# An expert stage's overflow branch, its scratch, four extra TensorE products and a table load change places in a two-layer MoE trunk

## The chip, the cores and the metric

The kernel runs on one core of a Trainium2 chip. The metric is the device time of one execution in microseconds; a profile of one execution shows each engine's instructions: TensorE (PE, with its weight loads as PEld), VectorE (DVE), ScalarE (ACT), GpSimd (POOL) and SyncE (SP), which here issues the weight transfers.

## The reference

256 tokens of 1024 numbers pass two layers. A layer is a token mixer (a gated depthwise convolution in the first, a chunked retention in the second), a norm, a mixture of 32 experts and another norm. All is float32. The part that the change touches is the mixture:

```python
grp_prob = softmax(xt @ w_grp + b_grp); p_g, g_idx = top_k(grp_prob, 1)      # 4 groups
exp_logits = (xt @ w_route + b_route).reshape(T, 4, 8)
sel = exp_logits of the chosen group; top_val, top_idx = top_k(sel, 2)
gates = softmax(top_val) * p_g
combine = sum(one_hot(g_idx * 8 + top_idx) * gates)                          # T x 32
for e in range(32):
    h = silu(xt @ w_gate[e]) * (xt @ w_up[e])                                # 1024 -> 512
    y = y + combine[:, e:e + 1] * (h @ w_down[e])                            # 512 -> 1024
x = layer_norm(alpha * x + y)
```

## The kernel before

Weights stream from memory in pieces of 1 MB (128 x 2048 float32), each into a slot of a ring of 12 or of a few other homes. The class that keeps them issues a load on SP as soon as a home is free: `take()` hands the next piece to the products, `used(n)` gives the homes of the n oldest pieces back and calls `load()` (L127 issues a whole piece, L112 one in halves). The engines' orders are those in which the code is written; nothing is moved by a scheduler.

An expert stage goes as follows. The routing (up to L1003) finds for each token its two experts. Three products, `pos` (L999 to L1001), give each token's place in its expert's list, with room for 64 tokens per expert. `one_hots` (L1043) makes from it, for four experts at a time, a selecting matrix on DVE. `gather` (L1057) multiplies it with the tokens, which are held as two parts `x1h` and `x1l`; four gathers make up the tokens of four experts, copied by ACT to `xghi` (gathers 0, 1) and `xglo` (gathers 2, 3). For each expert e `gate_up(e, i)`, i = 0 to 3, called product (e, i) here, does a quarter of both products (L1071, eight passes of 512 columns) into one accumulator `gu`; (e, 0) and (e, 1) read one pair of pieces, (e, 2) and (e, 3) the next. `hidden(e)` makes silu on ACT (L1080) and the product on DVE (L1082), `turn(e)` transposes the result on PE (L1091) and ACT copies it (L1104), `down` (L1126) multiplies with the third matrix, `parts` scales by the gates (ACT L1146, DVE L1147), and `scatter` (L1158) adds to the output rows. These steps of earlier experts are run between the products of later ones.

The list of an expert has 64 places. If one had more tokens, a second pass would be needed: `overflow`. `rest()`, called behind gathers 0 and 1, finishes the gates on DVE and returns `turned()`, called behind gathers 2 and 3: it transposes the places (`posT`, L1026) and, with a product (L1028), a sum and a cast on DVE (L1031, L1032), writes the number of tokens without a place to `flag`. `extra()`, called behind (0, 3), loads this number into a register of every engine (L1203) and opens `tc.If(rv > 0)` (L1208) around `overflow`. With the inputs of this kernel no list overflows, so the branch is never taken into the block. Its scratch are two ring slots (`spare`), and for their sake (0, 3) gives its two homes back only behind the branch. ACT then scales `cur`, the residual (L1228).

`warm(n, after)` (L302, L304) issues n bf16 products of 128 x 512 into a spare accumulator that nobody reads; `WARM` lists the n for eight places, and the sixth (`WARM[5]`, ahead of the gather) is 0. `preload(f)` (L361) calls a function of ACT on one column, so that ACT's function table is loaded ahead of its use; for the root it stands ahead of the norm that ends the stage.

Of the kernel before, what the change touches and what calls it, by code (L numbers as in the profile page):

```python
# [18 lines left out]
P = 128  # L19
# [14 lines left out]
T4 = 9  # L34
SPLIT = 4
ROWS_AT = [(27, 0), (27, 2), (28, 0), (28, 2)]
WARM = [11, 8, 8, 0, 2, 0, 1, 2]
YB = 2
TAPS_PE = [2, 2, 2, 2, 2, 2, 2, 14]
TAPS_POOL = [11, 12, 11, 8, 12, 11, 12, 7]  # L40
# [9 lines left out]
class Weights:  # L50
# [4 lines left out]
    def __init__(self, nc, ringp, splitp, handp, pieces, layers):  # L55
        self.nc, self.ringp, self.splitp, self.handp = nc, ringp, splitp, handp
        self.pieces, self.layers = pieces, layers
        self.next = 0
        self.tiles, self.parts = {}, {}
        self.order = [2 * i + j for i, (_, sp) in enumerate(pieces) if sp for j in range(2)]  # L60
        self.nsplit = 0
        self.nused = 0
        self.at = 0
        self.between = []
        self.stop = len(pieces)
        self.room = {"ring": RING, "own": 0, "split": 0, "once": 0}
        self.taken = []
        self.own = None

    def home(self, i):  # L70
        for a, b in self.layers:
# [19 lines left out]
    def load(self, n=99):  # L91

        for _ in range(n):
            while self.next in self.tiles:
                self.next += 1
            for i in range(self.next, len(self.pieces)):
                home, kind = self.home(i)
                if i not in self.tiles and (self.room[home] or home != "once"):
                    break
            else:  # L100
                return
            if not self.room[home]:
                return
            self.room[home] -= 1
            src = self.pieces[i][0]
            dma = self.nc.sync.dma_start
            if home == "split" or kind:
                m = src.shape[1] // 2
                v = []
                for h, tag in enumerate(("hd", "hd") if kind == "hand" else ("hi", "lo")):  # L110
                    t = (self.handp if kind == "hand" else self.splitp).tile([P, m, 1024 // m], F32, tag=tag, name=f"w{i}{h}")
                    dma(t, src[:, h * m:(h + 1) * m])  # L112
                    v += [t[:, k] for k in range(m)]
                self.tiles[i] = v
                continue
            t = (self.own if home == "own" else self.ringp).tile([P, 2048], F32, tag=home, name=f"w{i}",
                                                                 bufs=2 if home == "own" else RING)
            if isinstance(src, list):
                v = t.rearrange("p (g a b) -> p g a b", g=2, b=P)
                for g in range(2):  # L120
                    dma(v[:, g], src[g])
                    if self.between:
                        self.between.pop(0)()
                v = [v[:, g] for g in range(2)]
            else:
                v = t.rearrange("p (a b) -> p a b", a=src.shape[1])
                dma(v, src)  # L127
                if not self.pieces[i][1]:
                    v = [v[:, k] for k in range(src.shape[1])]
            self.tiles[i] = v  # L130
# [32 lines left out]
        t, self.tiles[i] = self.tiles[i], None  # L163
        return t

    def spare(self, name):

        t = self.ringp.tile([P, 2048], F32, tag="ring", name=name, bufs=RING)
        return t[:, 0:1024], t[:, 1024:2048]

    def used(self, n=1):

# [14 lines left out]
def trunk(ctx, tc, a, out):  # L187
# [18 lines left out]
    def sm1(name, dt=F32):  # L206
        return psum.tile([P, 512], dt, tag="sm", name=name, bufs=4)
# [740 lines left out]
    def route(L, ep, lg, comb, posm, posT, flag):  # L948
# [3 lines left out]
        def words(n):  # L952
            used[0] += n
            return space[:, used[0] - n:used[0]]

        def t2(n):
            t = words(2 * n)
            return t.rearrange("p (a b) -> p a b", a=2) if n > 1 else t

        def t2b():  # L960

            return words(NE).bitcast(BF).rearrange("p (a b) -> p a b", a=2)
# [43 lines left out]

        def rest():

            pg = t2(1)
            V.tensor_reduce(pg, gs, op=OP.add, axis=AX.X)  # L1010
            g1 = t2(1)
            V.scalar_tensor_tensor(g1, ex, 1.0, pg, op0=OP.add, op1=OP.mult)
            V.reciprocal(g1, g1)
            V.tensor_tensor(ex, ex, g1, op=OP.mult)
            V.tensor_tensor(oh1, oh1, bc(g1, 32), op=OP.mult)
            V.tensor_tensor(oh2, oh2, bc(ex, 32), op=OP.mult)
            V.tensor_tensor(comb, oh1, oh2, op=OP.add)
            posb = t2b()
            V.tensor_copy(posb, posm)
            over = t2b()  # L1020
            V.tensor_scalar(over, posm, CAP + 1.0, None, op0=OP.is_ge)

            def turned():
                pt = sm1("posT", BF)
                for tt in range(2):
                    PE.transpose(pt[:NE, tt * P:(tt + 1) * P], posb[:, tt], identb)  # L1026
                fp = sm1("flag")
                PE.matmul(fp[:1, 0:64], onesb[:, 0:1], over.rearrange("p a b -> p (a b)"), start=True, stop=True)  # L1028
                V.tensor_copy(posT, pt[:NE, :T])
                ff = words(1)[:1]  # L1030
                V.tensor_reduce(ff, fp[:1, 0:64], op=OP.add, axis=AX.X)  # L1031
                V.tensor_copy(flag, ff)  # L1032

            return turned

        mark["rest"] = rest

    def experts(L, mp, ep, x1h, x1l, comb, posm, posT, flag):
# [22 lines left out]
        def gate_up(e, i):  # L1061

            if i == 0:
                gus[e] = acc1(f"gu{e}")
            if i % 2 == 0:
                gws[e] = W.take(), W.take()
            for k in range(2):
                kt = i * 2 + k
                l = xg[e // 4][kt // 4][:, kt % 4, e % 4 * CAP:(e % 4 + 1) * CAP]
                for m, w in enumerate(gws[e]):  # L1070
                    PE.matmul(gus[e][m * CAP:(m + 1) * CAP], l, w[i % 2 * 2 + k], start=kt == 0, stop=kt == KT - 1)  # L1071
            if i % 2:
                gws.pop(e)
                if (e, i) != (0, 3):
                    W.used(2)

        def hidden(e):
            gu = gus.pop(e)
            gl = ep.tile([P, 512], F32, tag="gl", name=f"gl{e}")[CAP:]
            S.activation(gl, gu[:CAP], AF.Silu)  # L1080
            hs[e] = ep.tile([P, 4, P], F32, tag="h", name=f"h{e}")[CAP:]
            V.tensor_tensor(hs[e].rearrange("s k p -> s p k"), gl.rearrange("s (p k) -> s p k", k=4),  # L1082
                            gu[CAP:].rearrange("s (p k) -> s p k", k=4), op=OP.mult)
# [117 lines left out]
        def extra():  # L1201

            rv = nc.values_load(flag[0:1, 0:1], min_val=0, max_val=T * NE)  # L1203
            (wts, big), mid = [W.spare(f"ov{n}{L}") for n in range(2)]
            mid = [ep.tile([P, 512], F32, tag="gl", name="ovgl")[:CAP], *[m[:CAP] for m in mid]]
            row = ep.tile([P, T], F32, tag="s0", name="ovs", bufs=2)
            pair = [acc1(f"ov{n}") for n in range(2)]
            with tc.If(rv > 0):  # L1208
                overflow(L, x1h, x1l, comb, posm, wts, big, mid, row, pair)
        fin, seeds = {}, {}  # L1210
        identr = ep.tile([P, P], F32R, name="identr")
        G.tensor_copy(identr, ident)
        W.stop = layers[L][1]
        one_hots(0)
        warm(WARM[5])
        gather(0, range(2))
        turned = mark["rest"]()
        for e in range(NE):
            for i in range(4):
                gate_up(e, i)  # L1220
                if e == 0 and i == 0:
                    gather(0, range(2, 4))
                    turned()
                if e == 0 and i == 3:
                    extra()
                    W.used(2)
                    for tt in range(2):
                        S.activation(cur[:, tt], cur[:, tt], AF.Copy, scale=ALPHA)  # L1228
                if i == 3:
                    hidden(e)  # L1230
                run(e, i)
                if e + 4 < NE and e % 4 == 1 and i == 0:
                    one_hots(e // 4 + 1)
                if e + 2 < NE and e % 4 == 2:
                    gather(e // 4 + 1, [i])
                if (e, i) in ROWS_AT:
                    n = ROWS_AT.index((e, i))
                    if n == 0:
                        rows = mp.tile([P, 2048], F32, tag="x1h", name=f"rows{L}")
                    spread_rows(L, rows, n)  # L1240
            if L == 0 and e == 3:
                mark["rot"] = rotary_tables()
            if L == 0 and e == 10:
                mark["rot"]()
# [139 lines left out]
```

## Time and profile before

| | us |
|---|---|
| three runs | 1291.44, 1292.09, 1296.46 |
| median | 1292.09 |
| profiled execution | 1292.11 |
| its span | 1290.4 |
| PE busy | 1246.8 (97%) |
| DVE busy | 490.5 (38%) |
| ACT busy | 338.7 (26%) |

The profiled execution is the one whose rows are used; 1.7 us of its time lie outside the span. The mean granted TensorE clock was 0.98 of full speed. The two expert stages run from about 138 to 600 us and from about 821 to 1284 us. A table of stretches gives for each the engines' busy time, the granted clock and the share of the DMA engines; a timeline gives an engine's instructions with the idle time before each and what ended it.

### The profile page before, as it was taken

To read this page: it belongs to the slowest core of one execution; us is meant where nothing else is said; L and a number is where in the kernel's file an instruction comes from. 1 tells how busy PE (TensorE), PEld (TensorE's weight loads), DVE (VectorE), ACT (ScalarE), POOL (GpSimd) and SP (SyncE) were. 2 spreads that over 40 slices of the span, in tenths; PEclk is the share of its full clock that TensorE was granted. 3 is DMA by queue.
4 is the path that set the end of the run, shared out by engine and by line. 5 is a ranking of instruction groups with operands and counts; after the bars stand their busy time and mean duration, and the time that the engine had idled before them with its cause. 6 is when DMAs were issued, how large, how long until landed. Compare 5 with 4: busy or idle time off the path is not lost.

```text
span 1290.4 us, 15546 instructions
## 1 busy us (share of the span) xinstructions
PE 1246.8 (97%) x6163; PEld 659.6 (51%) x6163; DVE 490.5 (38%) x863; ACT 338.7 (26%) x561; POOL 139.9 (11%) x167
## 2 busy tenths in 40 slices
PE   9989899999999999998999999899999999999996
PEld 7867444343443334434997788544443444444432
DVE  5986313222232222235566755413222232222224
ACT  4655311121111111123434543411111211111111
POOL 4882008100000000002130000000000000000000
PEclk9999799999999999998999999899999999999998
DMA  9935699999999999999865556699999999999993
GB/s 321 398 116 175 224 391 426 425 425 425 424 427 425 425 425 425 426 427 409 290 197 180 179 196 197 261 382 405 422 425 426 425 427 425 425 426 424 427 426 137
DMA packets 102390, 459.45 MB, mean 356 GB/s; under 512 B 8258, under 2 KB 25442, under 8 KB 59554
## 3 DMA queue, kind: packets, MB, share of 16 engines
q1 hardware_dynamic: 102082, 457.92, 88.2%
q8 instruction: 53, 0.87, 0.3%
q0 software_dynamic: 80, 0.26, 0.1%
q10 hardware_dynamic: 144, 0.15, 0.1%
q14 instruction: 31, 0.25, 0.0%
HBM read 457.25 MB, written 1.05 MB: 355 GB/s over the span
## 4 chain that ended last, share of the span: by engine, by line
PE 60%; DMA 25%; DVE 2%; ACT 1%; issue 0%; DVEq 0%; SPq 0%; ACTq 0%
PE gu L1071 22%; DMA w<-in_moe_w_up_dram 11%; DMA w<-in_moe_w_down_dram 11%; PE y L1126 10%; PE gp L1057 4%; PE sc L1158 3%; DMA w<-in_moe_w_gate_dram 2%; PE vg L788 2%; PE vg L790 2%; PE vg L789 2%; PE hT L1091 1%; PE qk L771 1%; PE qk L770 1%; PE qk L768 1%; PE wo L656 1%; PE wo L657 1%
## 5 line engine op out<-in xcount | busy, mean ns | idle before, releaser
L1071 PE MATMUL gu<-w,xghi 128*64 128x512 f32 x1024 | 250.5, 606 | 1.9 <-DMA w<-in_moe_w_up_dram 1.0
L1126 PE MATMUL y<-w,h 128*64 128x512 f32 x960 | 240.9, 596 | 7.5 <-DMA w<-in_moe_w_down_dram 7.4
L1071 PE MATMUL gu<-w,xglo 128*64 128x512 f32 x1024 | 242.6, 600 | 0.0
L1082 DVE TENSOR_TENSOR h<-gl,gu 64x512 f32<-64x512 f32 x64 | 67.7, 1058 | 368.4 <-ACT gl L1080 368.4
L1126 PEld LDWEIGHTS y<-w,h 128*64 128x64 f32 x960 | 73.4, 137 | 151.8 <-issue 134.2
L1071 PEld LDWEIGHTS gu<-w,xglo 128*64 128x64 f32 x1024 | 69.7, 137 | 117.5 <-issue 107.9
L1071 PEld LDWEIGHTS gu<-w,xghi 128*64 128x64 f32 x1024 | 67.8, 137 | 110.4 <-issue 101.2
L143 DVE TENSOR_TENSOR l<-w,h 128x1024 fp32r<-128x1024 f32 x66 | 83.6, 1269 | 68.7 <-ACT h L142 67.1
L142 ACT ACTIVATE h<-w 128x1024 fp32r<-128x1024 f32 x72 | 75.7, 1058 | 88.0 <-PE vg L790 31.7
L1080 ACT ACTIVATE gl<-gu 64x512 f32<-64x512 f32 x64 | 37.7, 589 | 229.0 <-PE gu L1071 229.0
L1104 ACT ACTIVATE h<-hT 128x256 f32<-128x256 f32 x64 | 24.7, 385 | 261.3 <-PE hT L1101 148.9
L1162 DVE TENSOR_TENSOR cur<-sc,cur 128x512 f32<-128x512 f32 x112 | 69.5, 683 | 19.0 <-PE sc L1158 19.0
L1113 DVE COPY gsl<-hT 64x1 f32<-64x1 f32 x60 | 9.4, 156 | 169.8 <-ACT h L1104 169.4
L1057 PE MATMUL gp<-oh,x1h 128*128 128x256 f32 x256 | 59.0, 313 | 3.7 <-DVE route L1010 3.7
L1057 PEld LDWEIGHTS gp<-oh,x1h 128*128 128x128 f32 x256 | 40.5, 196 | 40.5 <-issue 39.6
L1146 ACT ACTIVATE yh<-y,gsl 128x512 fp32r<-128x512 f32 x60 | 41.2, 687 | 75.8 <-PE y L1126 75.6
L466 PE MATMUL pw<-xT,w 128*128 128x256 f32 x256 | 57.8, 381 | 1.6 <-DMA w<-in_conv_w_pw_dram 1.6
L499 POOL TENSOR_TENSOR gp<-gp,gt 128x256 f32<-128x256 f32 x76 | 56.3, 742 | 22.0 <-ACT gt L498 16.6
L143 POOL TENSOR_TENSOR l<-w,h 128x1024 fp32r<-128x1024 f32 x6 | 14.9, 2516 | 364.1 <-ACT h L142 364.1
L466 PEld LDWEIGHTS pw<-xT,w 128*128 128x128 f32 x256 | 48.2, 190 | 8.9 <-issue 2.5
L1057 PE MATMUL gp<-oh,x1l 128*128 128x256 f32 x256 | 52.6, 288 | 0.0
L1139 DVE TENSOR_SCALAR s<-sp,cc 128x256 fp32r<-128x256 f32 x30 | 14.5, 484 | 86.0 <-PE sp L1136 86.0
(322 smaller groups left out, 1585.1 us busy)
## 6 DMA issues: line engine op xcount, KB each, us to landing
w<-in_moe_w_up_dram SPq DMA_DIRECT2D x116, 1024.0 KB, 15.8
w<-in_moe_w_down_dram SPq DMA_DIRECT2D x112, 1024.0 KB, 17.1
w<-in_moe_w_gate_dram SPq DMA_DIRECT2D x106, 1024.0 KB, 14.7
w<-in_ret_w_qkvg_dram SPq DMA_DIRECT2D x24, 1024.0 KB, 13.2
w<-in_moe_w_gate_dram SPq DMA_DIRECT2D x44, 512.0 KB, 14.7
w<-in_moe_w_down_dram SPq DMA_DIRECT2D x32, 512.0 KB, 17.2
w<-in_moe_w_up_dram SPq DMA_DIRECT2D x24, 512.0 KB, 17.2
w<-in_conv_w_pw_dram SPq DMA_DIRECT2D x16, 512.0 KB, 6.3
```

What stands on the lines that cost most here:

```text
L142: self.nc.scalar.activation(hi, w, AF.Copy)
L143: (self.nc.gpsimd if pool else self.nc.vector).tensor_tensor(lo, w, hi.bitcast(F32), op=OP.subtract)
L466: PE.matmul(ps[:, 1 - g], w[g][:, kt], xT[:, kt], start=kt == 0, stop=kt == KT - 1)
L499: G.tensor_tensor(gps[c], gps[c], t, op=OP.add)
L1057: PE.matmul(ps[:, k], src[:, tt, q * 2 + k], o[:, tt].rearrange("p e c -> p (e c)"), start=i == 0, stop=i == 3)
L1071: PE.matmul(gus[e][m * CAP:(m + 1) * CAP], l, w[i % 2 * 2 + k], start=kt == 0, stop=kt == KT - 1)
L1080: S.activation(gl, gu[:CAP], AF.Silu)
L1082: V.tensor_tensor(hs[e].rearrange("s k p -> s p k"), gl.rearrange("s (p k) -> s p k", k=4), gu[CAP:].rearrange("s (p k) -> s p k", k=4), o ...
L1126: PE.matmul(ys[pr][b][j * CAP:(j + 1) * CAP], hs[e][:, kt], wds[e][kt % 2][:, n * 512:(n + 1) * 512], start=kt == 0, stop=kt == 3)
L1146: S.activation(yh[:, n], ys[pr][n], AF.Copy, scale=g)
L1158: PE.matmul(ps, s0[pr][ks, tt * P:(tt + 1) * P], ys[pr][i][ks, n if pr >= 0 else 0], start=not held and i == 0, stop=i == 1 and (pr == -1 ...
L1162: V.tensor_tensor(o, ps, o, op=OP.add)
```

## The change

`WARM[5]` goes from 0 to 4. The sum for the flag, `over`, is made first in `rest()`, the flag's product is a function of its own (`flagged`), called right behind gather 0, and `extra()` with the branch stands behind gathers 1 and 2, ahead of product (0, 0). Gather 3 and the transposes of the places follow (0, 1). The scratch is no longer two fresh slots but three homes whose pieces are already loaded (`lend`); inside the branch, after `overflow`, these pieces are read again. (0, 3) gives its homes back at once. A `preload(AF.Sqrt)` is added behind the last `hidden`.

```diff
-WARM = [11, 8, 8, 0, 2, 0, 1, 2]
+WARM = [11, 8, 8, 0, 2, 4, 1, 2]
...
-    def spare(self, name):
-
-        t = self.ringp.tile([P, 2048], F32, tag="ring", name=name, bufs=RING)
-        return t[:, 0:1024], t[:, 1024:2048]
+    def lend(self, n):
+
+        held = sorted(i for i, v in self.tiles.items() if v is not None and i in self.raw)[-n:]
+        return [self.raw[i] for i in held]
...
+            over = t2b()
+            V.tensor_scalar(over, posm, CAP + 1.0, None, op0=OP.is_ge)
             pg = t2(1)
...
-            over = t2b()
-            V.tensor_scalar(over, posm, CAP + 1.0, None, op0=OP.is_ge)
+
+            def flagged():
+                fp = sm1("flag")
+                PE.matmul(fp[:1, 0:64], onesb[:, 0:1], over.rearrange("p a b -> p (a b)"), start=True, stop=True)
+                ff = words(1)[:1]
+                V.tensor_reduce(ff, fp[:1, 0:64], op=OP.add, axis=AX.X)
+                V.tensor_copy(flag, ff)
...
-                if (e, i) != (0, 3):
-                    W.used(2)
+                W.used(2)
...
-            (wts, big), mid = [W.spare(f"ov{n}{L}") for n in range(2)]
-            mid = [ep.tile([P, 512], F32, tag="gl", name="ovgl")[:CAP], *[m[:CAP] for m in mid]]
+            lent = W.lend(3)
+            (wts, big), mid, (sg, _) = [(t[:, 0:1024], t[:, 1024:2048]) for t, _, _ in lent]
+            mid = [sg[:CAP, 0:512], *[m[:CAP] for m in mid]]
...
                 overflow(L, x1h, x1l, comb, posm, wts, big, mid, row, pair)
+                for _, v, src in lent:
+                    nc.sync.dma_start(v, src)
...
-        gather(0, range(2))
-        turned = mark["rest"]()
+        flagged, turned = mark["rest"]()
+        gather(0, [0])
+        flagged()
+        gather(0, [1, 2])
+        extra()
         for e in range(NE):
             for i in range(4):
                 gate_up(e, i)
-                if e == 0 and i == 0:
-                    gather(0, range(2, 4))
+                if e == 0 and i == 1:
+                    gather(0, [3])
                     turned()
                 if e == 0 and i == 3:
-                    extra()
-                    W.used(2)
                     for tt in range(2):
                         S.activation(cur[:, tt], cur[:, tt], AF.Copy, scale=ALPHA)
                 if i == 3:
                     hidden(e)
+                    if e == NE - 1:
+                        preload(AF.Sqrt)
```

PE at the head of the first expert stage. `gp00` to `gp03` are the accumulators of gathers 0 to 3, `gu0` that of expert 0. Before:

```order
L1001 MATMUL pos_1265<-route0_1225,triub_153 128x32
L1057 MATMUL gp00_1278<-oh0_1274,x1h_1108 128x256 x2
L1057 MATMUL gp01_1288<-oh0_1274,x1l_1109 128x256 x2
L1071 MATMUL gu0_1307<-w12_205,xghi0_1276 64x512
L1057 MATMUL gp02_1312<-oh0_1274,x1h_1108 128x256 x2
L1028 MATMUL flag_1335<-route0_1225,onesb_126 1x64
L1071 MATMUL gu0_1307<-w15_400,xglo0_1277 64x512
L1203 TENSOR_LOAD flag_1113
L1208 COMPARE_AND_BRANCH
```

Now, at the same place:

```order
L1004 MATMUL pos_1265<-route0_1225,triub_153 128x32
L307 MATMUL warm_1276<-onesb_126 128x512
L1062 MATMUL gp00_1292<-oh0_1274,x1h_1108 128x256 x2
L1028 MATMUL flag_1302<-route0_1225,onesb_126 1x64
L1062 MATMUL gp01_1306<-oh0_1274,x1h_1108 128x256 x2
L1062 MATMUL gp02_1316<-oh0_1274,x1l_1109 128x256 x2
L1207 TENSOR_LOAD flag_1113
L1213 COMPARE_AND_BRANCH
```

Of each kind of row only the first or last is shown (four `warm` rows, eight rows a pair of gathers). All of expert 0's products stood ahead of the branch; now only gathers 0 to 2 do.

SP in the same place, whose loads are named by piece. Before:

```order
L112 DMA w291_1223<-in_moe_w_down_dram 128x1024
L127 DMA w31_1344<-in_moe_w_up_dram 128x2048
L127 DMA w32_1346<-in_moe_w_gate_dram 128x2048
L1203 TENSOR_LOAD flag_1113
L1208 COMPARE_AND_BRANCH
L127 DMA w33_1730<-in_moe_w_up_dram 128x2048
L127 DMA w34_1732<-in_moe_w_gate_dram 128x2048
```

Now:

```order
L113 DMA w291_1223<-in_moe_w_down_dram 128x1024
L1207 TENSOR_LOAD flag_1113
L1213 COMPARE_AND_BRANCH
L128 DMA w31_1709<-in_moe_w_up_dram 128x2048
L128 DMA w32_1711<-in_moe_w_gate_dram 128x2048
L128 DMA w33_1735<-in_moe_w_up_dram 128x2048
L128 DMA w34_1737<-in_moe_w_gate_dram 128x2048
```

The rows of the block that isn't entered are left out. Pieces 31 and 32, which wait for (0, 1), moved behind the branch.

ACT at the end of the second expert stage. `gl` is the last silu, `yh` the scaled results, `h` the copy for `down`, `lnm10sd` the norm's root. Before:

```order
L1080 ACTIVATE gl31_8906<-gu31_8828 64x512
L1146 ACTIVATE yh-2_8914<-y-20_8884,gsl-2_8848 128x512
L1104 ACTIVATE h3231_8927<-hT31_8918 128x256
L1146 ACTIVATE yh-1_8940<-y-10_8931,gsl-1_8929 128x512
L361 ACT_TABLE_LOAD
L361 ACTIVATE pre_8960<-epsc_149 128x1
L342 ACTIVATE lnm10sd_8967<-lnm10mv_8965,epsc_149 128x1
```

Now:

```order
L1084 ACTIVATE gl31_8918<-gu31_8840 64x512
L364 ACT_TABLE_LOAD
L364 ACTIVATE pre_8922<-epsc_149 128x1
L1150 ACTIVATE yh-2_8928<-y-20_8896,gsl-2_8860 128x512
L1108 ACTIVATE h3231_8941<-hT31_8932 128x256
L1150 ACTIVATE yh-1_8954<-y-10_8945,gsl-1_8943 128x512
L364 ACTIVATE pre_8974<-epsc_149 128x1
L345 ACTIVATE lnm10sd_8981<-lnm10mv_8979,epsc_149 128x1
```

The table load moved ahead of the scaled results and of `h`; at its old place the small activation stays.

## Rows read from the trace of the kernel before

**Rows 1.** Page: DMA engines' busy share, in 40 slices of the span.

```profile
DMA  9935699999999999999865556699999999999993
```

**Rows 2.** Stretches: start and end, length, busy us, PEclk, DMA share, GB/s.

```profile
137.90:143.10 5.20, 5.14 (x20) 4.02 (x22) 1.19 (x8) 1.20 (x2) 0.00 (x0) 0.50 0.40 160
143.20:149.00 5.80, 5.80 (x37) 3.16 (x35) 0.55 (x3) 1.35 (x3) 0.00 (x0) 1.00 0.01 1
155.20:160.20 5.00, 4.95 (x20) 2.16 (x22) 1.00 (x3) 0.39 (x1) 0.00 (x0) 0.66 0.33 77
191.00:194.00 3.00, 3.00 (x14) 1.45 (x11) 1.60 (x2) 0.59 (x1) 0.00 (x0) 1.00 0.87 264
200.00:240.00 40.00, 40.00 (x204) 16.84 (x200) 8.81 (x15) 6.68 (x12) 29.77 (x38) 1.00 1.01 425
816.00:825.80 9.80, 7.95 (x34) 5.78 (x35) 5.46 (x24) 1.40 (x3) 0.00 (x0) 0.50 0.71 288
838.00:842.00 4.00, 4.00 (x24) 1.84 (x24) 1.00 (x3) 0.38 (x1) 0.00 (x0) 1.00 0.28 53
```

**Rows 3.** Waits of the load queue, 160 to 240 us: total, times, longest.

```profile
SPq L127 <- PE gu L1071: 48.0, 10, 6.9
```

**Rows 4.** PE timeline, first head: start, us, what [idle before <-releaser].

```profile
134.30 1.01 PE L304 MATMUL warm<-onesb 128*128 128x512 bf16 x2
...
135.91 0.19 PE L1001 MATMUL pos<-route,triub 128*128 128x32 bf16 x1
137.96 0.77 PE L1057 MATMUL gp<-oh,x1h 128*128 128x256 f32 x2 [1.86 <-DVE route L1010]
...
141.64 2.66 PE L1071 MATMUL gu<-w,xghi 128*64 128x512 f32 x8
144.23 0.51 PE L1057 MATMUL gp<-oh,x1h 128*128 128x256 f32 x2
...
146.31 0.28 PE L1026 MATMUL posT<-identb,route 128*32 128x128 bf16 x2
```

**Rows 5.** Flag, branch and what follows, timelines of DVE, ACT, PE; instruction queue (148:152).

```profile
147.08 0.14 DVE L1032 CAST flag<-route 1x1 int32<-1x1 f32 x1
...
148.84 1.28 ACT L1228 ACT_TABLE_LOAD   x1 [1.83 <-DVEq L1208]
...
152.11 1.94 PE L1071 MATMUL gu<-w,xghi 128*64 128x512 f32 x8 [0.19 <-PEq L1208]
...
829.76 0.14 DVE L1032 CAST flag<-route 1x1 int32<-1x1 f32 x1
...
831.00 1.28 ACT L1228 ACT_TABLE_LOAD   x1 [1.31 <-DVEq L1208]
...
835.26 1.94 PE L1071 MATMUL gu<-w,xghi 128*64 128x512 f32 x8 [0.66 <-PEq L1208]
...
q8 instruction: 1, 0.02, 1.6%
```

**Rows 6.** PE timeline: first turn and product (1, 1) of the first layer.

```profile
155.25 0.43 PE L1091 MATMUL hT<-ident,h 64*128 64x64 f32 x4 [1.20 <-DVE h L1082]
...
156.15 3.10 PE L1071 MATMUL gu<-w,xghi 128*64 128x512 f32 x8
```

**Rows 7.** Timeline of the second stage's end, ACT and PE.

```profile
1271.34 0.69 ACT L1146 ACTIVATE yh-2_8914<-y-20_8884,gsl-2_8848 128x512 fp32r<-128x512 f32 x1 [1.13 <-PE y-20_8884 L1126]
...
1272.21 0.38 ACT L1104 ACTIVATE h<-hT 128x256 f32<-128x256 f32 x1 [0.18 <-PE hT L1096]
...
1272.65 3.65 PE L1126 MATMUL y-10_8931<-w,h 128*64 128x512 f32 x16 [0.49 <-ACT h L1104]
...
1277.05 1.28 ACT L361 ACT_TABLE_LOAD   x1
...
1278.35 0.20 ACT L361 ACTIVATE pre<-epsc 128x1 f32<-128x1 f32 x1
...
1279.98 0.29 ACT L342 ACTIVATE lnm10sd<-lnm10mv,epsc 128x1 f32<-128x1 f32 x1 [1.43 <-DVE lnm10mv L340]
```

More of the change, by code (lines that the diff above doesn't have):

```diff
@@ L68, in __init__ @@
         self.own = None
+        self.raw = {}
     def home(self, i):
@@ L127, in load @@
                 dma(v, src)
+                if home == "ring":
+                    self.raw[i] = t, v, src
                 if not self.pieces[i][1]:
@@ L1026, in turned @@
                     PE.transpose(pt[:NE, tt * P:(tt + 1) * P], posb[:, tt], identb)
-                fp = sm1("flag")
-                PE.matmul(fp[:1, 0:64], onesb[:, 0:1], over.rearrange("p a b -> p (a b)"), start=True, stop=True)
                 V.tensor_copy(posT, pt[:NE, :T])
[L1030 to L1034, printed above, removed]
+            return flagged, turned
         mark["rest"] = rest
```

## The prediction

> **What bounds the kernel now.** I read the page's busy shares by slice first: the DMA share stands at 9 through both expert stages [rows 1]. The table of stretches then shows the steady part: from 200 to 240 us DMA is full at 425 GB/s [rows 2]. So an expert stage ends when its weights have come in, and an edit ahead of it counts only if it lets transfers start earlier or keeps the DMA engines from running dry. They do run dry early in the stage, at 191 to 194 (share 0.87) [rows 2], and the waits of the load queue say why: between 160 and 240 its largest wait by far is for PE's gate products, 48.0 us in 10 waits [rows 3]. A weight slot is loaded again only when PE has read it. In this stretch (about 160 to 203 us) PE paces the loads, and what PE gains or loses ahead of it, the end gains or loses.
>
> Then the head of the stage, which the edit rewrites. PE ends the position products at 136.1 and starts the gather at 137.96 after 1.86 us of idling [rows 4]. From 137.9 to 143.1 the granted clock is 0.50 (1.2 GHz of 2.4), and 1.00 from 143.2 on; the second layer's head, 816 to 825.8, is at 0.50 too [rows 2]. The branch stands behind product (0,3). Between the flag's cast and ScalarE's next work lie 148.84 − 147.22 = 1.62 us in the first layer and 831.00 − 829.90 = 1.10 in the second, but PE has queued work meanwhile and idles only 0.19 and 0.66 us there [rows 5].
>
> **Part 1, four warm products.** They fill the idle 1.86 us. What half clock costs in the head: gathers 0 and 1 took 141.64 − 137.96 = 3.68 us, gathers 2 and 3 at full clock 146.31 − 144.23 = 2.08; product (0,0) took 2.66 against 1.94 at full clock [rows 4, 5]. That is 1.60 + 0.72 = 2.3 us a layer, the ceiling of the gain; the floor is 0, if the clock rises no earlier. In between: the rows show the clock back at full 5.1 us after PE took up work at 137.96, and 5.0 us after it did at 155.25 [rows 2, 4, 6]. With the hole filled PE has worked without a hole from 136.1, so the like rise would come at 141.2. The short dip is the other end: a mean of 0.66 over the 5.0 us from 155.2 is 2 × 0.34 × 5.0 = 3.4 us at half clock [rows 2], and 136.1 + 3.4 = 139.5. Each us at half clock loses half of itself, so the gain is (143.1 − 141.2)/2 = 1.0 to (143.1 − 139.5)/2 = 1.8 us; I take the middle, **1.4 us a layer**. The products themselves lie in idle time: two of this kind took 1.01 us at half clock [rows 4], so four take at most 2.02 and delay the gather by at most 0.16, which I count as nothing.
>
> **Part 2, the branch ahead of product (0,0).** At its old place it costs PE nothing that comes back: after (1,0) PE waits anyway for hidden(0), 1.20 us before 155.25 [rows 6], because ScalarE's table load and gate function start only when (0,3) ends. Taking 0.19 or 0.66 us out ahead of that wait makes the wait longer. At the new place the branch has less cover. Gather 0 ends at about 137.96 + 1.84 = 139.8; the flag's product, sum and cast take some 0.7 us, so the flag is there at 140.5, and engines pass the branch 1.10 to 1.62 us later: 141.6 to 142.1. Gathers 1 and 2, which PE holds as cover, take 1.04 each at full clock and 1.84 at half, and end at 141.9 (full from 139.8 on) to 142.5 (from 141.2 on). So the flag is just covered, and the old price of 0.19 to 0.66 is open. Above that, one 16 KB instruction transfer shows right behind the branch [rows 5]; at the old place it lay under the queued products, now nothing lies over it. Bounds: 0.2 us (the smaller gap), and 1.6 us (the whole time from flag to passage open). Nearest to the new place is neither, since half the cover is gone: **0.9 us a layer**. Below nothing is not possible, as a branch that was covered goes to a place with less cover. Queued behind it: on PE all of expert 0; on ScalarE gather 3's copy behind one table load (1.28), needed only by (0,2), two products of 1.94 later; on DVE nothing until hidden(0); on GpSimd nothing that anyone waits for in the head.
>
> The Trainium skill, "Runtime: NRT & Kernel Launch", section "Instruction fetch mechanics", says that a taken branch whose target lies outside the two pages held makes the sequencer fetch by DMA before it goes on. The one transfer of 0.02 MB behind the branch [rows 5] agrees; by that rule the upper bound of 1.6 us would be the likelier value, and the sum below would stand 2 × 0.7 = 1.4 us later.
>
> **Part 3, the loads around the branch.** Before, SP issued its first two loads just ahead of the branch and passed it only when they had landed, and only then issued the next. DMA was busy 0.33 of 155.2 to 160.2, an idle of 5.0 × 0.67 = 3.4 us, and 0.28 of 838 to 842, 2.9 us [rows 2]. Now these loads come behind the branch, no transfer is under way there, and the two held back for the scratch go out at (0,3)'s end. Four pieces land earlier. But the pieces after them wait for PE's reads as before, and DMA, which finds nothing to do at times around 191 already [rows 2], would stand that much more idle there. I count **0**; the other answer is a rival. The reloads of borrowed homes are inside the branch and don't run.
>
> **Part 4, root's table.** The table load and its little activation (1.28 + 0.20, with gaps 1.51 us) now follow the last gate function, which ends at 1271.34 − 1.13 = 1270.21. ScalarE is then free at 1271.75, not 1271.34, so yh-2 comes 0.41 later and ends 1272.44; h, which ran at 1272.21, goes to 1272.46. PE's y-10 had waited 0.49 us for just that h [rows 7]: 0.25 later. At the old place nothing comes back: the load ran 1277.05 to 1278.33 and the root at 1279.98 waited for DVE's mean and variance [rows 7]. Cost **+0.25 us a layer, 0.5 in all**, between 0 and 0.8 (two times 0.41).
>
> **The sum**, against the profiled run of 1292.1 us, which is the median too: 2 × (−1.4 + 0.9) + 0.5 = −0.5: **1291.6 us**. A faster or slower kernel by under 0.5% (6.5 us) can't be told from no change by a measurement, so this is "same". With the ends of the two terms (gain 1.0 to 1.8, price 0.3 to 1.4) it is 1289.8 to 1293.4. One more thing is open: the dip that the 1.20 us of idling before 155.25 brought (eight passes in 3.10 us against 1.94 [rows 5, 6]), worth 3.4/2 = 1.7 us. The second layer had none (1.00 in 838 to 842 [rows 2]). It may go in the first or come in the second, 1.7 either way: 1288.1 to 1295.1.
>
> **Rivals.** *A, the branch stands open.* PE has no work but two gathers over the branch; if the passage and the instruction transfer take 1.6 us in the open, that hole is as long as the 1.86 us which kept the clock at half before, and the gain of part 1 is lost as well: 2 × 1.6 + 0.5 = +3.7, 1295.8 us. Should the clock then fall again in both layers, another 2 × 1.7: 1299.2, which is slower than before by a measurable amount. It decides from a PE loss of 3.0 us a layer (2 × 3.0 + 0.5 = 6.5). For it: the transfer behind the branch. Against: PE's small gaps at the old place. *B, the change does not do what it says:* the hole is filled but the clock rises where it rose; branch at its old mean price, 0.4: 2 × 0.4 + 0.5 = +1.3, 1293.4. For it: from 816 to 820.7, with warm products on PE, the clock stood at 0.50 as well [rows 2]. *C, the idle DMA comes through:* 3.4 + 2.9 us of idle transfers vanish and are not given back: −6.3 − 1.0 + 0.5 = −6.8, 1285.3, faster. For it: the stage ends by DMA. Against: the 48.0 us of waits for PE and the dry places behind [rows 2, 3]. *D, the table costs ScalarE double:* yh-2 and h wait as long again as the load, 1.28 us a layer: +2.6 on the forecast, 1294.2. Against: the activation after the old load started 0.02 us behind it (1277.05 + 1.28 to 1278.35 [rows 7]). The Trainium skill, "ScalarE: Activation LUTs", section "What ACT_TABLE_LOAD costs", gives a drain of about 1380 ns besides the load of 1283 ns; the trace agrees on the load and shows no such drain behind it.
>
> **How the numbers follow.** Forecast 0.45; A 0.22, of which 0.05 beyond 1298.6; B 0.20; C 0.09; D 0.04. The range leaves out C and the end of A: 1288.0 to 1297.0. Faster by over 0.5% is most of C and a little of the forecast with both gains at their ends, 0.08; slower is A's end, 0.05; the rest, 0.87, is the same.
>
> **What will show it.** Right: the idle before the first gather gone; the head at full clock from 139.5 to 141.2; PE's idle ahead of (0,0) near 0.9 us; loads behind (0,1) and (0,3) with no gap in DMA until 160, and more of it at 175 to 200; y-10 0.25 us later after ScalarE's h. Wrong: an expert stage that starts later and yet ends earlier by over 3 us (C), a hole of 1.6 us or more ahead of (0,0) with a clock of 0.50 behind it (A), a head at 0.50 to 143 (B).

## The result, and the profile after

| | before | changed |
|---|---|---|
| median of 8 runs, us | 1295.49 | 1300.99 |
| lowest, highest | 1291.44, 1297.09 | 1296.82, 1303.52 |
| span of the profiled execution | 1290.4 | 1296.3 |

The ratio is 1.0051 with a 95% interval of [1.0034, 1.0068]: the changed kernel is slower by half a percent (6.6 us by this ratio, 5.5 us between the medians), and the forecast of no change did not hold. The median of the eight runs before is 3.4 us above that of the three runs that the prediction started from, so by ratio the forecast was 0.9996 and its range 0.997 to 1.004; 1.0051 lies outside either way.

PE's timeline at the head of the first expert stage, in the changed kernel (start, length, what, idle before and what ended it), which answers to [rows 4, 5]:

```profile
137.47 0.19 PE L1004 MATMUL pos<-route,triub 128*128 128x32 bf16 x1
137.50 1.15 PE L307 MATMUL warm<-onesb 128*128 128x512 bf16 x4
139.53 0.47 PE L1062 MATMUL gp<-oh,x1h 128*128 128x256 f32 x2 [0.88 <-DVE route L1013]
...
142.50 0.40 PE L1062 MATMUL gp<-oh,x1l 128*128 128x256 f32 x2
146.48 3.65 PE L1076 MATMUL gu<-w,xghi 128*64 128x512 f32 x16 [3.59 <-PEq L1213]
```

And of the second stage:

```profile
827.03 0.40 PE L1062 MATMUL gp<-oh,x1l 128*128 128x256 f32 x2
830.42 5.35 PE L1076 MATMUL gu<-w,xghi 128*64 128x512 f32 x16 [2.99 <-PEq L1213]
```

The last column is the result: PE stands idle for 3.59 and 2.99 us ahead of product (0, 0), released by its own sequencer at the branch. In the second stage the 16 passes behind the hole take 5.35 us, where the first takes 3.65. The table of stretches (columns as in [rows 2]) gives the clock beside it:

```profile
139.50:142.90 3.40, 3.36 (x25) 3.01 (x25) 1.51 (x10) 1.20 (x2) 0.00 (x0) 1.00 0.60 240
142.90:146.40 3.50, 0.00 (x0) 0.00 (x0) 0.00 (x0) 1.88 (x2) 0.00 (x0) 1.00 0.06 14
155.00:160.00 5.00, 3.60 (x22) 1.53 (x20) 1.36 (x4) 2.25 (x3) 0.00 (x0) 1.00 1.01 406
175.00:200.00 25.00, 25.00 (x126) 10.27 (x126) 6.71 (x11) 4.51 (x8) 3.80 (x5) 1.00 0.90 347
824.00:827.40 3.40, 3.40 (x26) 3.03 (x25) 1.52 (x11) 1.20 (x2) 0.00 (x0) 1.00 0.20 80
830.50:835.70 5.20, 5.20 (x17) 1.68 (x17) 0.00 (x0) 0.00 (x0) 0.00 (x0) 0.67 0.02 3
```

The gathers now run at full clock in both layers (1.00 where [rows 2] have 0.50). In the hole ScalarE works (1.88 us of 3.50), and SyncE has nothing to issue until (0, 1) gives its homes back. Behind the hole of the second stage the clock falls (0.67 as a mean of 830.5 to 835.7).

No view shows the branch itself, but the trace has the records of the sequencers. The compare-and-branch instruction, in us (start, length):

```
            before L0       before L1       changed L0      changed L1
TensorE     148.40  3.36    831.12  3.98    142.16  4.01    826.50  3.60
ScalarE     147.98  0.04    830.48  0.04    143.70  0.04    828.20  0.04
VectorE     148.13  0.07    830.66  0.06    142.16  0.07    826.52  0.06
GpSimd      148.32  0.04    830.53  0.04    142.36  0.04    826.40  0.04
SyncE       150.78  0.05    833.00  0.05    142.70  0.05    826.60  0.05
```

PE's branch takes 3.4 to 4.0 us at either place. Before, 3.60 us of passes of (0, 2) and (0, 3) lay queued over it, and only 0.19 or 0.66 us showed:

```profile
148.32 3.60 PE L1071 MATMUL gu<-w,xglo 128*64 128x512 f32 x16
...
831.00 3.60 PE L1071 MATMUL gu<-w,xglo 128*64 128x512 f32 x16
```

Now PE has 0.7 and 0.9 us of gathers left when the branch starts. In each of the four a 16 KB instruction transfer on DMA queue 8 begins 1.0 to 1.1 us after the branch does (149.43, 832.13, 143.21 and 827.61). By the counts this queue carries TensorE's instructions: from 200 to 560 us of the kernel before it has 14 such transfers for 3512 TensorE rows, and no other engine has more than 326 rows there.

SyncE's short record does not show all of its delay: in the changed kernel its next record begins 3.07 and 2.93 us after the branch has ended. Nothing waited for it here, since SyncE issues its next load at 150.13, when (0, 1) ends.

The two profiled spans differ by 5.9 us, and not all of that is the change. 1.55 us are there ahead of the first routing, in identical instructions. From the first layer's `pos` to its steady part (200 us) the changed kernel loses nothing: the offset goes from 1.56 to 1.26, since the hole stands against a head at full clock and the dip of [rows 6], which did not come. The second layer's router product ran at half clock in this execution (3.63 us, before 1.98), +1.65; its head, from the gather's start to (1, 1), lost 2.65. Such falls of the clock ahead of the stage differ from execution to execution, so the parts were told apart by repeated runs.

### The profile page after: what moved, and what is told of

The parts are those of the page before. It is cut to its first block, busy times and chain, and to the rows that moved or that the text cites. A ratio compares the mean times of both kernels' runs of the same rounds, so it can differ in the third digit from the quotient of the medians.

```text
span 1296.3 us, 15569 instructions
## 1 busy us (share of the span) xinstructions
PE 1246.1 (96%) x6171; PEld 659.7 (51%) x6171; DVE 490.8 (38%) x863; ACT 338.1 (26%) x563; POOL 139.4 (11%) x167
## 5 line engine op out<-in xcount | busy, mean ns | idle before, releaser
L1166 DVE TENSOR_TENSOR cur<-sc,cur 128x512 f32<-128x512 f32 x112 | 69.6, 684 | 18.9 <-PE sc L1162 18.9
```

The source lines that it names most:

```text
L1166: V.tensor_tensor(o, ps, o, op=OP.add)
```

## The experiments

The theory: the whole loss is PE's branch, open for 3.6 and 3.0 us, because the way over the block needs an instruction transfer; the warm products do what they are for. The rivals: the loss lies in the table load, in the warm products or in the loads, or the branch is long for another reason than its distance. All ratios are to the kernel before, with a 95% interval.

**Without the branch** (the overflow pass is left out).

```diff
         gather(0, [1, 2])
-        extra()
```

> The changed kernel without the flag's register load and without the branch (the overflow pass is left out altogether). Theory: the loss is PE's branch standing open ahead of product (0,0), 3.59 and 2.99 us in the profile of the changed kernel; without it PE goes from gather 2 straight to (0,0), the hole is under 0.3 us, and with the clock gain of the warm products kept the time is 6 to 9 us under the changed kernel, about 0.998 to 1.000 of the kernel before. Rival (the loss is elsewhere, in the table load at the end or in the routing's clock): the time stays within 2 us of the changed kernel, 1.004 to 1.006.

0.9983 [0.9971, 0.9995], 1291.95 us. The loss is the branch: with it 1.0051, without 0.9983, a difference of 0.0068 or 8.8 us. The two holes are 6.6 us and the fall of the clock behind the second 1.7, together 8.3. PE goes from gather to product without a hole:

```profile
144.21 0.40 PE L1062 MATMUL gp<-oh,x1l 128*128 128x256 f32 x2
144.54 1.94 PE L1076 MATMUL gu<-w,xghi 128*64 128x512 f32 x8
```

**The block cut to a third** (two of the three passes over places beyond 64 are left out of it).

```diff
-            for r in range(1, T // CAP):
+            for r in range(1, 2):
```

> The changed kernel with the block that is never entered cut to a third (one of three places passes; PE's loop body 72 instead of 216 instructions in the listing). Theory that PE's branch is long because its target lies many instructions away and must be fetched: PE's branch falls from 3.6 to 4.0 us to under 1.5, the hole ahead of (0,0) from 3.59 and 2.99 to under 1.3 us, and the time to about 1.000 to 1.002 of before. Rival that the price is that of the flag's way into PE's register and of PE's own drain, whatever lies in the block: the hole stays at 3 us or more and the time at 1.004 to 1.006.

1.0038 [1.0019, 1.0056]. Half of the expectation came: PE's branch took 1.07 us in the first layer and 3.33 in the second. PE's timeline, first and second layer:

```profile
143.95 1.51 PE L1076 MATMUL gu<-w,xghi 128*64 128x512 f32 x6 [0.65 <-ACT xglo L1064]
...
829.11 1.88 PE L1076 MATMUL gu<-w,xghi 128*64 128x512 f32 x4 [2.78 <-PEq L1213]
```

The instruction queues in the 1.07 us of the first branch, then in the 3.33 us of the second (packets, MB, share):

```profile
q14 instruction: 2, 0.02, 3.6%
...
q8 instruction: 1, 0.02, 1.8%
```

The long branch has a transfer of queue 8 in it, 1.02 us after its start (826.42); the short one has none. So it is the transfer that makes it long, and the block's length alone doesn't tell whether one is needed. The other runs bear this out: in all 15 PE branches of 3.33 us or more the branch ends 1.3 to 1.5 us after such a transfer does, whether the transfer takes 0.94 us or 1.85.

**The block emptied** (all its passes are left out).

```diff
-            for r in range(1, T // CAP):
+            for r in range(1, 1):
```

> The changed kernel with the block that is never entered emptied but for two small copies and the reloads (its passes are left out), so that PE has under 30 instructions to skip. In the cut to a third PE's branch took 1.07 us in the first layer but 3.33 in the second. Theory that it is the instruction transfer for a far target: PE's branch takes under 1.2 us in both layers, the holes ahead of (0,0) shrink to 0.3 to 0.8 us, and the time is 0.999 to 1.001 of before. Rival that the second layer's hole has another cause (the flag, the clock, PE's own drain): it stays near 3 us there, and the time at 1.003 to 1.004.

0.9972 [0.9959, 0.9986], 1291.88 us. PE's branch takes 0.24 and 0.21 us, with no packet of an instruction queue in it, and lies wholly under the gathers; SyncE's next record begins 0.14 and 0.13 us after its branch instead of 3.07 and 2.93. PE in the first layer:

```profile
145.18 0.40 PE L1062 MATMUL gp<-oh,x1l 128*128 128x256 f32 x2
145.51 1.08 PE L1076 MATMUL gu<-w,xghi 128*64 128x512 f32 x4
```

Flag, register load and branch are all there at the new place, and the loss is gone: the rival of the flag's way or PE's drain falls. What is dear is the jump over a block for which PE must fetch.

**The branch behind product (0, 1)**, ahead of its loads, with the full block.

```diff
         gather(0, [1, 2])
-        extra()
...
-                W.used(2)
+                if (e, i) != (0, 1):
+                    W.used(2)
...
                 if e == 0 and i == 1:
+                    extra()
+                    W.used(2)
                     gather(0, [3])
```

> The changed kernel with the branch behind product (0,1), ahead of its two loads and of gather 3, with the full block. Theory that the 16 passes of (0,0) and (0,1), 3.65 us, cover PE's branch of 3.4 to 4.0 us: the hole behind (0,1) is 0 to 1 us, SP still issues pieces 31 and 32 behind the branch without a wait for transfers, and the time is that without a branch plus up to 2 us: 0.998 to 1.000 of before. Rival that PE can't run ahead far enough there, because (0,0) waits for ScalarE's copies: the hole is 2 us or more and the time 1.003 or more.

1.0001 [0.9991, 1.0011]. The holes were longer than expected:

```profile
143.77 3.65 PE L1076 MATMUL gu<-w,xghi 128*64 128x512 f32 x16
149.06 0.48 PE L1062 MATMUL gp<-oh,x1h 128*128 128x256 f32 x2 [1.64 <-PEq L1214]
```

PE's branch began at 144.79 and took 3.96. The 16 passes end at 147.42, so they covered 2.6 us of it, not 3.65: the sequencer reached the branch 1.0 us after the first pass had begun. In the second layer 1.34 us were open. Cover works, and what counts is the work still queued when the branch begins.

**Without the warm products.**

```diff
-WARM = [11, 8, 8, 0, 2, 4, 1, 2]
+WARM = [11, 8, 8, 0, 2, 0, 1, 2]
```

> The changed kernel without the four warm products (0 as before). Theory that they do what they are for and only the branch costs: the idle before the first gather is back at 1.8 us, the clock is half in more of the head, gathers 0 to 2 take up to 5.5 instead of 3.0 us and the time rises by 2 to 5 us, to 1.006 to 1.009 of before. Rival that the warm products bring nothing here: within 1 us of the changed kernel, 1.005.

1.0060 [1.0038, 1.0082], against 1.0051 not told apart. Its profile says why so little is lost:

```profile
146.86 0.63 PE L1062 MATMUL gp<-oh,x1l 128*128 128x256 f32 x2
148.97 1.51 PE L1076 MATMUL gu<-w,xghi 128*64 128x512 f32 x6 [1.48 <-PEq L1213]
```

At half clock the gathers last longer and cover more of the branch: the hole is 1.48 us (1.52 in the second layer), not 3.59 and 2.99. In the changed kernel the warm products shorten the cover of a wait, so that by the profiles 2.1 and 1.5 us of their gain go into a longer hole. What is left of the gain the times don't tell.

**The kernel before with the warm products alone.**

```diff
-WARM = [11, 8, 8, 0, 2, 0, 1, 2]
+WARM = [11, 8, 8, 0, 2, 4, 1, 2]
```

> The kernel before with the four warm products alone. By the prediction's term they give back 1.0 to 1.8 us a layer: 0.997 to 0.9985 of before. Rival that the clock does not rise earlier or that it is lost behind: 0.9995 to 1.001.

0.9965 [0.9953, 0.9976], 1289.39 us: faster than both kernels: 0.35% are 4.5 us, somewhat more than the 2.0 to 3.6 us expected, though the interval reaches down to 3.1. Its head in the first layer:

```profile
141.12 0.48 PE L1057 MATMUL gp<-oh,x1h 128*128 128x256 f32 x2 [0.40 <-DVE route L1010]
...
143.16 0.65 PE L1071 MATMUL gu<-w,xghi 128*64 128x512 f32 x2
```

```profile
141.10:153.10 12.00, 11.61 (x67) 6.15 (x67) 1.74 (x11) 5.82 (x8) 0.00 (x0) 1.00 0.26 78
821.90:834.70 12.80, 11.98 (x68) 6.48 (x67) 1.74 (x11) 6.38 (x8) 0.00 (x0) 0.97 0.30 103
```

Both gathers are over 2.04 us after the start, where [rows 4] have 3.68, and the clock is 1.00 and 0.97.

**The kernel before without the branch** (the overflow pass is left out).

```diff
                 if e == 0 and i == 3:
-                    extra()
                     W.used(2)
```

> The kernel before without the flag's register load and the branch (the overflow pass is left out). By the prediction's term the old place costs the end nothing, since the PE gaps of 0.19 and 0.66 us lie ahead of a wait and the idle transfers there are paid back behind: 0.999 to 1.000 of before. Rival that the idle transfers of 3.4 and 2.9 us come through when nothing drains SP: 0.995 to 0.997.

1.0001 [0.9987, 1.0015]. The old place cost nothing that can be measured, neither by PE's small gaps nor by the idle transfers that SP's wait made.

**The root's table load.** Out of the changed kernel, and alone in the kernel before.

```diff
                 if i == 3:
                     hidden(e)
-                    if e == NE - 1:
-                        preload(AF.Sqrt)
```

> The changed kernel without the added load of the root's table (the one ahead of the norm makes it, as before). Theory: y-10 starts 0.25 us earlier per layer, the time falls by 0.5 us, within what can be measured, 1.0045 to 1.005. Rival that the table load moved into the last stage is a main part of the loss: the time falls by 2 us or more, to 1.0035 or less.

1.0072 [1.0055, 1.0090]. Without the load the kernel is not faster; the two intervals overlap, and the sign is against every case.

```diff
                 if i == 3:
                     hidden(e)
+                    if e == NE - 1:
+                        preload(AF.Sqrt)
```

> The kernel before with the added table load for the root alone. By the prediction's term y-10 comes 0.25 us later per layer, 0.5 us in all: 1.000 to 1.001 of before. Rival that ScalarE pays for the table twice (1.28 us more a layer, 3.1 us in all): 1.002 to 1.0025. The changed kernel without this load was not faster but 1.0072 [1.0055, 1.009] of before, so a gain by the load (0.998 to 0.999) is a third case.

0.9994 [0.9980, 1.0009]: no effect that can be told, and not the 1.002 of a table paid for twice.

**The head in each profile.** From the end of the position products to expert 0's first turn, in us, in the first and the second layer:

| kernel | first | second |
|---|---|---|
| before | 19.15 | 18.99 |
| before, without the branch | 19.08 | 19.12 |
| before, with the root's table load | 19.05 | 19.21 |
| before, with the warm products | 16.48 | 16.77 |
| changed | 20.54 | 21.39 |
| changed, without the branch | 16.57 | 16.89 |
| changed, block cut to a third | 17.28 | 21.19 |
| changed, block emptied | 16.99 | 16.89 |
| changed, branch behind (0, 1) | 19.42 | 18.01 |
| changed, without the warm products | 20.64 | 20.75 |
| changed, without the root's table load | 20.32 | 21.46 |

The warm products take 2.7 and 2.2 us out of the heads of the kernel before. In the changed one the first head is 0.1 us shorter with them and the second 0.6 us longer. The branch puts 4.0 and 4.5 us into the changed one, and 0.7 and 4.3 us when the block is cut to a third.

## Why the prediction was wrong

**The bound of the stage** held. SP's waits for PE's gate products from 160 to 240 us are as in [rows 3]:

```profile
SPq L128 <- PE gu L1076: 49.0, 10, 6.9
```

**Part 1, warm products:** the mechanism was right and the term too small. I took 1.4 us a layer with 1.8 as the upper end, and put the ceiling at 2.3. Alone they give 0.35% (4.5 us in two layers, 2.3 a layer, the ceiling itself, if the interval of 0.24% to 0.47% is read at its middle; its ends are 1.6 and 3.0 us a layer): the clock was back by the first gather (in the first layer) or within it. What I had mis-sized was the rise. I had let it come 3.4 to 5.1 us after 136.1, the end of the position products. The trace's record of the granted clock has it 0.1 and 1.5 us after their end in the changed kernel, and from 0.5 us before to 3.8 us after it in the 14 stages of all profiles with the warm products; in the eight stages without them it comes 6.9 to 7.8 us after.

**Part 2, the branch:** this is the step that made the forecast wrong. I bounded its price by 0.2 and 1.6 us a layer and took 0.9; it is 3.59 and 2.99 us open, and 3.4 to 4.0 us in all. The 1.6 us were ScalarE's time from flag to next work, put down for every engine. PE's own was in [rows 5] too: the flag's cast ended at 147.22 and PE's first product behind the branch began at 152.11, 4.9 us later (835.26 − 829.90 = 5.4 in the second layer); since PE stood idle just before, released by its sequencer, that is the sequencer's time and not that of the passes. ScalarE was through at 148.84 and 831.00, so 3.3 and 4.3 us of that were PE's alone. I read the idle of 0.19 and 0.66 us as the price, and it was what 3.60 us of queued passes had left of it. The other half of the step was right: the flag came in time (cast ended at 141.25, PE's branch began at 142.16, the last gather ended at 142.90):

```profile
141.11 0.14 DVE L1031 CAST flag<-route 1x1 int32<-1x1 f32 x1
```

The rule of the Trainium skill that I had set beside it ("Runtime: NRT & Kernel Launch", section "Instruction fetch mechanics": a taken branch to a target that is not at hand has to fetch first) agrees with the traces: every one of PE's branches of 3.3 us or more had a 16 KB transfer of queue 8 in it, and those of 0.2 and 1.07 us had none. Whether the target lay outside what was held no record shows. I gave it an upper end of 1.6 us from the wrong row.

**Part 3, the loads:** right in its sum. SyncE passed the old branch at 150.78 and waited for the two transfers right behind it (its next load went out at 157.89), not ahead of it as I had it; for the loads that comes to the same. No transfer gap stands at 155 to 160 (share 1.01 where [rows 2] have 0.33), the DMA engines idle later instead (0.90 from 175 to 200, before 0.98), and the kernel before without SP's wait is no faster (1.0001). The stretch before:

```profile
175.00:200.00 25.00, 25.00 (x124) 9.94 (x122) 6.70 (x11) 3.92 (x7) 5.30 (x7) 1.00 0.98 381
```

**Part 4, the table load:** a small term, forecast at +0.25 us a layer and measured at none. ScalarE at the stage's end, to be read beside [rows 7]:

```profile
1275.47 0.59 ACT L1084 ACTIVATE gl<-gu 64x512 f32<-64x512 f32 x1 [8.96 <-PE gu L1076]
1276.08 1.28 ACT L364 ACT_TABLE_LOAD   x1
...
1277.38 0.20 ACT L364 ACTIVATE pre<-epsc 128x1 f32<-128x1 f32 x1
1277.48 0.67 ACT L1150 ACTIVATE yh-2_8928<-y-20_8896,gsl-2_8860 128x512 fp32r<-128x512 f32 x1
...
1278.06 0.38 ACT L1108 ACTIVATE h<-hT 128x256 f32<-128x256 f32 x1
...
1278.50 3.65 PE L1130 MATMUL y-10_8945<-w,h 128*64 128x512 f32 x16 [0.49 <-ACT h L1108]
```

From gate function to h it is 2.59 us, as before, and y-10 waits the same 0.49. I had added the pieces end to end; here yh-2 starts 0.10 us after the little activation does and h 0.09 us before yh-2 ends. The drain that "ScalarE: Activation LUTs", section "What ACT_TABLE_LOAD costs", in the Trainium skill gives besides a table load is not seen here either: the load starts 0.02 us after the gate function ends, and the next activation 0.02 us after the load.

**The rivals.** A (the branch open, the clock down behind it) is what happened, in kind: a loss beyond the forecast, with the clock falling in the second layer. Its price per branch was half of the real one, and its premise that the hole takes the gain of part 1 away did not hold: the gathers kept their full clock, and the gain went into a longer hole. The time by A's own end, 1299.2 from 1292.1, is a ratio of 1.0055; that this is near the 1.0051 measured is luck, since its terms (1.6 us a branch, the clock down in both layers) are not those measured (3.59 and 2.99 us, and in one layer). B is refuted (the clock rose earlier), C by the kernel before without the branch, D by the table load alone.

**The sum and the dip.** The price's ends of 0.2 and 1.6 became 0.3 and 1.4 in the sum without a reason given, and 2 × (−1.8 + 0.3) + 0.5 = −2.5 gives 1289.6, not 1289.8. Neither changes the outcome. I also took half a percent for what can't be measured; the intervals here are 0.1% to 0.2% to either side. The dip of [rows 6] is there in the first layer in five of the eleven profiles (the kernel before, and the changed one without the branch, with the block at a third, with the branch behind (0, 1) and without the warm products) and in the second layer in none. The 1.20 us of idling that I blamed isn't enough: in the changed kernel PE idled 1.40 us at that place in both layers, and the clock stayed at full.

**What stays open:** why the block at a third of its length needs a transfer in one layer and not in the other. In the first layer queue 8 had last begun a transfer 1.7 us before the branch, in the second 18.9 us before; where the code of the two layers lies against what the sequencer holds was not varied by itself. The heads, too, are not the whole difference in time: against the kernel before they are 3.8 us longer in the changed kernel, where the ratio gives 6.6 us, and 4.7 us shorter without the branch, where the ratio gives 2.2. No run separates what makes up these 2.5 to 2.8 us (the order of gather 3 and the transposes, the borrowed scratch, falls of the clock elsewhere).

## What to carry to other kernels

The gap that a profile shows behind a branch is its price less the work that lay queued over it; before such an instruction is moved, take the time from its condition to the first work behind it, on the engine in question and not on another, and set the cover of the new place against that. A branch over a block like this one wants long work queued on TensorE when it begins, or a block short enough that nothing has to be fetched. An edit that speeds up the cover of a wait can lose its gain again: here the warm products pay 0.35% alone, and ahead of the open branch a gain that can't be told from none. So the fastest of these kernels that keeps the overflow pass whole is the old one with them, 0.9965 [0.9953, 0.9976].

## What the runs showed of the hardware

The compare-and-branch that is written once in the program takes 0.04 to 0.07 us in the records of four engines. On TensorE it takes 3.3 to 4.2 us when a 16 KB transfer of queue 8 falls into it (15 branches), 1.07 us over the block cut to a third where none does, and 0.21 to 0.24 us over the emptied block. With the transfer, the branch ends 1.3 to 1.5 us after it; the transfer begins 0.9 to 1.5 us after the branch does and takes 0.9 to 1.9 us.

That TensorE alone pays is not shown. The body of the block has 216 rows on TensorE and 217 on SyncE in the program's listing, and at most 52 on the others. SyncE stands still as well, behind its record, though what it waits for no record shows: its next record begins 2.9 to 3.1 us after the branch in the changed kernel, and 0.13 to 0.14 us after it over the emptied block. VectorE's next begins 0.2 to 0.5 us after in the changed kernel, ScalarE's and GpSimd's 0.1 to 0.4 us.
